# A planner's rough duration of a float32r TensorE pass, set to the measured one, in a two-layer hybrid trunk step

## The chip, the cores and the metric

One core of one Trainium2 chip. The metric is device time in microseconds (us), median of the runs shown. In views of the profile PE is TensorE's matmuls, PEld its weight loads, DVE is VectorE, ACT ScalarE, POOL GpSimd, SP SyncE.

## The reference, cut to what matters

Two trunk layers run over 128 context tokens and 256 latent tokens, 1024 wide (T = 384 tokens side by side in the kernel). Each layer is a macaron of three residual parts, every one modulated by nine vectors computed from a condition:

```
mod = silu(cond) @ w_mod[l] + b_mod[l]            # 1024 -> 9 * 1024, per layer and condition
x = x + 0.5*g1 * swiglu(m(rmsnorm(x)), w1, w3, w2)     # 1024 -> 2816 -> 1024
x = x + g2 * mixer_l(m(rmsnorm(x)))
x = x + 0.5*g3 * swiglu(m(rmsnorm(x)), w1, w3, w2)
```

The mixer of layer 0 (even) is a bidirectional gated linear recurrence beside differential attention of 4 heads; that of layer 1 (odd) is windowed grouped-query attention with 16 heads and sink logits. Both have one input and one output projection. Outputs are y for both token groups and the context keys, values and states.

## The kernel before, in words

**Layout.** x lies transposed: 8 tiles of 128 features by 384 tokens. A weight tile is 128 by 128. Every weight is split into a float32r high part (`hi`) and a low part (`lo`), and so is every x operand, and one product takes three float32r passes of 384 columns (386 where two columns for the shift ride along): hi*hi, hi*lo, lo*hi (`mm3`, line 436). Products of small operands inside the mixers (norm sums, gates, context scores, attention times values) are plain float32.

**Stages, in order.** The start computes the first modulation vectors. Then come `ffn(0,0)`, `even_mixer`, `ffn(0,1)`, `ffn(1,0)`, `odd_mixer`, `ffn(1,1)`. In the profiled execution they run at about 36 to 316, 316 to 482, 482 to 757, 757 to 1041, 1041 to 1188 and 1188 to 1460 us. An `ffn` (line 602) has an up pass of 22 tiles, each 16 `mm3` (48 passes) into one of two `sc` PSUM tiles, and a down pass of 8 tiles of 22 `mm3` (66 passes) into one of two `mm` PSUM tiles.

**Weights.** 156 chunks of 1 MB arrive on SP's queue in the order in which the program reads them (`w_load`, DMA on line 387). A group of 8 weight tiles is split by `w_split` (line 391): a 1024-column copy to `hi`, mostly on ACT, and a 1024-column subtraction to `lo` on DVE. Four groups are held; splitting runs three groups ahead of the matmuls.

**Modulation.** 128 tiles of `w_mod`, 0.5 MB each, arrive on POOL's queue, and DVE reduces each one twice (`mod_one`, line 476; tile `junk`, two conditions). Each reduction waits for `DVE_IDLE`, that is, it is written where the planner thinks that DVE has at most 0.6 us of work queued. These reductions are written during the FFNs only, up to tile 6 of the down pass.

**The order of the written program.** Each engine executes its instructions in the order written, and waits at the first whose inputs are missing. That order is chosen while the program is written. `Clock` (line 83) keeps a rough time at which each engine falls free and each tile is ready; `Eng.cost` (line 229) gives a rough duration for each instruction; a result is usable on another engine 0.2 us later (`HOP`). `Sched.now()` (line 127) is the planned time of TensorE. After each `mm3` or small matmul, `tick` (line 164) goes through the side chains (evacuations, norms, attention heads, weight splits, modulation) and writes up to six of their stages whose inputs are, on this clock, ready by `now()`. A side chain's own matmuls (call them pieces) are thus put between passes of the main stream. `ffn`, `proj_pass` and `out_pass` also ask the clock: from which tile on the normed x is used instead of the scaled x (`direct`), and which output tile comes next.

The lines of `cost` for TensorE and DVE, and of `tick`:

```python
        if self._name == "PE":
            if op == "transpose":
                return 0.109
            n = k["rhs"].free_size()
            if k["rhs"].dtype in (F32R, BF16):
                return n * 0.000417 + 0.0035
            us = max(n, 128) * 0.00168
            return us * max(out.shape[0], 32) / 128
...
        if op in self.SLOW:
            m = max([v.free_size() for v in ins] + [n]) if op != "tensor_tensor_reduce" else ins[0].free_size()
            return 0.065 + col + 0.00104 * m
...
    def tick(self):
        if not self.busy:
            n = 0
            while n < 6 and self._poll(self.now()):
                n += 1
```

Every compute instruction is issued through `Eng`, so nearly all rows of the profile have line 214; tiles tell them apart. Slab tiles are named `s` whatever they hold.

Names used below. `normed_all` (line 560) makes the normed x, eight features in turn, two SCALAR_TENSOR_TENSOR on DVE each, waiting for the norm (`RS.ev`) and `DVE_IDLE`. `evac` (line 687) empties an `mm` tile of the projection. `qk_norm` (line 714) has one piece of two passes against `cst`, and a shift by a DMA from `s` to `s` that the planner counts as 3.0 us. `a_chain` (lines 1099, 1182) writes scores, a maximum, exponentials, sums, and 128-column transposes against `ident`. `o_chain` (lines 1123, 1210) is attention times values.

Of the kernel before, what the change touches and what calls it, by code (L numbers as in the profile page):

```python
# [17 lines left out]
PSUM = bass.MemoryType.PSUM  # L18
# [27 lines left out]


class Event:
    """Something that a chain of instructions has still to emit, with the tiles that it leaves."""

    def __init__(self):
        self.tiles = None


class Banks:
    """PSUM tiles of one tag: how many may be in use at a time, and when the free ones fell free."""

    def __init__(self, n):
        self.at = [0.0] * n


class Idle:
    """Ready when an engine has nothing else queued."""

    def __init__(self, eng):
        self.eng = eng
# [14 lines left out]


class Clock:
    """Rough times of the engines while the program is written: they order the emission and nothing else."""

    def __init__(self):
        self.free = dict.fromkeys(("PE", "ACT", "DVE", "POOL", "DMA"), 0.0)
# [29 lines left out]


class Sched:
    """Emits the stages of side chains between pieces of the matmul stream, each when its inputs should be there."""  # L120

    def __init__(self):
        self.clock = Clock()
# [76 lines left out]


class Eng:
    """An engine's instructions, timed by the clock as they are written."""

    SLOW = {"tensor_tensor", "scalar_tensor_tensor", "tensor_tensor_scan", "tensor_reduce", "tensor_tensor_reduce"}

# [22 lines left out]
    def cost(self, op, out, ins, k):  # L229
        n = out.free_size()  # L230
        ps = any(v.space == PSUM for v in ins)
        if self._name == "PE":
            if op == "transpose":
                return 0.109
            n = k["rhs"].free_size()
            if k["rhs"].dtype in (F32R, BF16):
                return n * 0.000417 + 0.0035
            us = max(n, 128) * 0.00168
            return us * max(out.shape[0], 32) / 128
        if self._name == "ACT":  # L240
            extra = sum(0.093 for n_ in ("scale", "bias", "accum_out") if hasattr(k.get(n_), "tensor"))
            return 0.093 + 0.000833 * n + extra + (-0.042 if ps else 0.0)
        col = 0.064 if any(hasattr(v, "tensor") and v.free_size() == 1 for v in ins[1:]) else 0.0
        if self._name == "POOL":
            return 0.06 + 0.0007 * n
# [3 lines that stand above are left out]
        if op == "reciprocal":  # L249
            return 0.065 + 0.0083 * n  # L250
        return 0.065 + col + (0.00104 if ps else 0.00052) * n


def emit(tc, D, order):
    nc = tc.nc
    ctx = ExitStack()
    with ctx:
# [12 lines left out]
        clock = sched.clock  # L270
# [49 lines left out]
            S_.activation(out, in_, func, **kw)  # L320

        def copy(out, in_, scale=None):
            """out = in_ (times a column), on the engine that should be done with it first."""
            k = {} if scale is None else {"scale": scale}
            r = max(clock.at(in_)[0], clock.at(out)[0])
            ta = max(clock.free["ACT"], r) + S_.cost("activation", out, [in_], k)
            td = max(clock.free["DVE"], r) + V.cost("tensor_copy", out, [in_] if scale is None else [in_, scale], k)
            if td + ON_ACT < ta:
                if scale is None:
                    V.tensor_copy(out, in_)  # L330
                else:
                    V.tensor_scalar(out, in_, scale, None, ALU.mult)
            else:
                act(out, in_, AF.Copy, **k)

# [1 line left out]
        scT = cpool.tile([P, KD, 32], F32, name="scT")  # L337
        craw = cpool.tile([P, KD, 2], F32, name="craw")
        nc.sync.dma_start(craw, D["c_cols"])
# [8 lines left out]
        x = [sl() for _ in range(KD)]  # L348
# [19 lines left out]
            o = PPC[name][0] + i  # L368
            return pp[:, o:o + 1]

# [1 line left out]
        class WS:  # L372
            raw, hi, lo, rest = {}, {}, {}, {}
            asked, due = set(), []
# [69 lines left out]
            TE.matmul(ps, lhsT=lhsT, rhs=rhs, start=start, stop=stop)  # L444
            sched.tick()

# [1 line left out]
        M = {}  # L448
        mod_todo = [(0, k, t) for k in range(2, 9) for t in range(8)] + [(1, k, t) for k in range(9) for t in range(8)]
        mod_tiles = {}  # L450
# [23 lines left out]
                V.tensor_scalar(m, m, 0.5, None, ALU.mult)  # L474

        def mod_one():
            """Generator: one modulation tile, a condition per stage."""
            i = mod_at[0]
            l, k, t = mod_todo[i]
            mod_at[0] += 1  # L480
            if t == 0:
                M[l, k] = cpool.tile([P, 8, 2], F32, name=f"M{l}_{k}")
            w = mod_tiles.pop(i)
            for c in range(2):
                yield DVE_IDLE, w
                junk = modp.tile([P, 1024], BF16, tag="junk", name=nm("junk"), bufs=1)
                V.tensor_tensor_reduce(out=junk, in0=w, in1=cbc[:, c, :], scale=1.0, scalar=0.0,
                                       op0=ALU.mult, op1=ALU.add, accum_out=M[l, k][:, t, c:c + 1])
            mod_load()
            if t == 7:  # L490
                mod_finish(l, k)
                mod_done.add((l, k))
# [17 lines left out]
                sched.busy = was  # L510
            return M[l, k]

# [1 line left out]
        class XS:  # L514
            hi, lo, ev, sq, A, sh = [], [], [], None, None, None

# [3 lines left out]
            XS.hi, XS.lo, XS.sq, XS.ev = [None] * KD, [None] * KD, None, [Event() for _ in range(KD)]  # L520

        def prep(d, with_sh=True):
            """Generator: scaled x as two float32r parts, and the sum of squares."""
            q = sl()
            hi = XS.hi[d] = sl(F32R, TB)
            lo = XS.lo[d] = sl(F32R, TB)
            act(q, x[d], AF.Square)
            for r, c in RANGES:
                copy(hi[:, r], x[d][:, r], XS.A[:, d, c:c + 1])
            if with_sh:  # L530
                copy(hi[:, T:TB], XS.sh[:, d, :])
            yield hi, q
            if XS.sq is None:
                XS.sq = q
            else:
                V.tensor_tensor(XS.sq, XS.sq, q, ALU.add)
            for r, c in RANGES:
                V.scalar_tensor_tensor(lo[:, r], x[d][:, r], XS.A[:, d, c:c + 1], r32(hi[:, r]), ALU.mult, ALU.subtract)
            if with_sh:
                V.tensor_tensor(lo[:, T:TB], XS.sh[:, d, :], r32(hi[:, T:TB]), ALU.subtract)  # L540
            sched.fire(XS.ev[d], hi, lo, XS.sq)

        class RS:
            t, ev = None, None
# [13 lines left out]
            sched.add(gen(RS.t, RS.ev, XS.ev))  # L558

        def normed_all(low):  # L560
            """Starts the chains that leave the normed and modulated x as two float32r parts."""
            xn = [None] * KD
            xn_ev = [Event() for _ in range(KD)]
            A, sh, rs_ev, rs = XS.A, XS.sh, RS.ev, RS.t
# [33 lines left out]
                yield from prep(d)  # L598
            sched.add(gen())

# [1 line left out]
        def ffn(l, n, nxt):  # L602
            sched.fire(mod_on)
            gkind = 2 if n == 0 else 8
# [78 lines left out]
            h[0], h[1] = hh, hl  # L683
            sched.fire(h[2], hh, hl)

# [1 line left out]
        def evac(ps, direct):  # L687
            t = sl()
            if direct:
# [22 lines left out]
        sig_done = Event()  # L712

        def qk_norm(t, bc, gate, gs):
            """Generator: leaves the normed rows in t, then returns the two parts of the rotated ones."""
            sq = sl()
            if bc is None:
                act(sq, t, AF.Square)
# [102 lines left out]
            sched.add(gen())  # L821

        def transposed(src, n):
            """w (128 queries, n*128 keys) -> SBUF (keys, n, queries)."""
            pt = mst()
            for b in range(n):
                TE.transpose(pt[:, b * P:(b + 1) * P], src[:, b * P:(b + 1) * P], ident)
            w = sl()
            copy(w[:, :n * P], pt[:, :n * P])
            free(msb, pt, w)  # L830
            return w
# [13 lines left out]
            return ps, n  # L845

        def proj_pass(tiles, key, done, low):
            """Projection tiles in order; the first two share a K order that leaves the last tile of x late."""
            i = 0
            xn, xn_ev = normed_all(low) if low < 5 else (None, [Event() for _ in range(KD)])  # L850
            direct = False
# [27 lines left out]
                    i += 1  # L879

        def out_pass(key, gm, nxt, ready, free_at, early, wide):
            """Output projection. The K tiles in `early` come first: x takes their part while the others are computed."""
            prep_begin(*nxt)
            gm = mod_need(*gm)
            late = [k for k in range(KD) if k not in early]
# [3 lines left out]
            borrowed = set()  # L889

            def slot(t, ps):
                """A bank that has nothing to do: kept while there are units to come."""
                if todo:
                    slots.append((t, ps))
                else:
                    (msb if ps.tensor.name in borrowed else mmb).at.append(t)
# [61 lines left out]
            ready[k][0], ready[k][1] = hh, hl  # L958
            sched.fire(ready[k][2], hh, hl)

# [1 line left out]
        def even_mixer(nxt):  # L962
            mod_on.tiles = None
            rstd_chain()
# [203 lines left out]
            proj_pass(tiles, "e_in", done, XN_E)  # L1168
            out_pass("e_out", (0, 5), nxt, ready, [ready[k][2] for k in range(4, 8)], [4, 5, 6, 7], WIDE_E)

# [1 line left out]
        def odd_mixer(nxt):  # L1172
            mod_on.tiles = None
            rstd_chain()
# [65 lines left out]
            proj_pass(tiles, "o_in", done, XN_O)  # L1240
            out_pass("o_out", (1, 5), nxt, ready, [ready[k][2] for k in range(8)], list(range(O_EARLY)), WIDE_O)

# [1 line left out]
        def wm_load(i):  # L1244
            t = rawp.tile([P, 2, 1024], F32, tag="raw", name=nm("wm0"))
            nc.sync.dma_start(t, D["wm0"][i])
# [2 lines left out]

        def mixer_consts():  # L1250
            yield RS.ev, el, pp
            # differential lambda, negated
            V.tensor_scalar(gsub, par("subln"), 1.0 - LAM_INIT, None, ALU.mult)
            lj = sl()
            for m in range(2):
                V.tensor_tensor_reduce(out=lj[:, 0:64], in0=el[:, 2 * m, :], in1=el[:, 2 * m + 1, :], scale=1.0, scalar=0.0,
                                       op0=ALU.mult, op1=ALU.add, accum_out=ls[:, m:m + 1])
            # -8 * softplus(-lam) on (128, 2 directions, 4 tiles); log1p by its series in z / (2 + z)
            lam = pp[:, PPC["lam"][0]:PPC["lam"][0] + 8]
            V.tensor_scalar(sa, lam, -1.0, None, ALU.mult)  # L1260
            V.tensor_tensor(sb, lam, sa, ALU.min)
# [85 lines left out]
        sched.drain()  # L1347


# order of the 64 rows of a q or k head on the partitions: the two rows of a rotary pair side by side  # L1350
ROPE = np.array([b + i + s for b in (0, 32) for i in range(16) for s in (0, 16)])
UNROPE = np.argsort(ROPE)

# [133 lines left out]
```

## Time and profile before

| | |
|---|---|
| median of 3 runs | 1465.27 us (1465.2 to 1465.8) |
| profiled execution, span from first to last instruction | 1464.2 us (its own time is not listed apart from the runs) |
| TensorE busy | 1436.7 us, 98% |
| VectorE busy | 1115.4 us, 76% |
| ScalarE busy | 659.8 us, 45% |
| granted TensorE clock, mean | 0.997 |
| bytes moved by DMA | 250.67 MB, 171 GB/s |

How to read it: busy time is the time in which an engine had an instruction at work. A matmul's duration overlaps with the next one's, so the pace of the stream is read from how many passes stand in a stretch. The waits view lists time in which an engine had nothing at work, and what ended it. The windows view gives busy time of each engine in a stretch, with its instruction count in brackets.

### The profile page before, as it was taken

Reading aid. Unit: us, or ns where it says so; the run is one execution under the profiler, and the core shown is the slowest. Engines: PE = TensorE matmul, PEld = TensorE weight load, DVE = VectorE, ACT = ScalarE, POOL = GpSimd, SP = SyncE. Lnnn points to the kernel's source line nnn. Section 1 sums busy time; section 2 is a strip of 40 time slices with the busy share of each in tenths; the row PEclk is TensorE's granted clock in tenths of the full one; section 3 lists DMA queues with packets and bytes.
Section 4 is the critical chain, followed back from the end, with each engine's and each line's share of the span. In section 5 each row is a group of like instructions: output and inputs, shape, how many; then the busy total and the mean of one; then the engine's idle time right before and its main releaser. Section 6 shows DMA issues by size and latency. Waiting matters only on the chain.

```text
span 1464.2 us, 21823 instructions
## 1 busy us (share of the span) xinstructions
PE 1436.7 (98%) x8354; PEld 1398.4 (96%) x8354; DVE 1115.4 (76%) x2103; ACT 659.8 (45%) x1193; POOL 103.8 (7%) x214
## 2 busy tenths in 40 slices
PE   4999999999999999999999999999999999999998
PEld 1999999998889999999999999999998899999998
DVE  3899999969998998999979997444698795444332
ACT  3643333348875633333345333333477664333321
POOL 0001111110220011111100110000100000000000
PEclk9999999999999999999999999999999999999999
DMA  9557767652322366766744766333331233333430
GB/s 361 216 185 257 246 245 257 235 173 101 120 99 97 140 230 236 254 243 231 254 177 153 251 243 196 135 119 130 117 107 51 77 120 115 133 126 116 146 135 22
DMA packets 49560, 250.67 MB, mean 171 GB/s; under 512 B 6464, under 2 KB 10960, under 8 KB 28336
## 3 DMA queue, kind: packets, MB, share of 16 engines
q1 hardware_dynamic: 29664, 180.05, 34.0%
q0 software_dynamic: 19792, 69.23, 14.2%
q8 instruction: 66, 1.08, 0.3%
q14 instruction: 38, 0.31, 0.1%
HBM read 244.53 MB, written 2.36 MB: 169 GB/s over the span
## 4 chain that ended last, share of the span: by engine, by line
PE 95%; DMA 2%; DVE 2%; ACT 1%; issue 0%; SPq 0%; DVEq 0%; ACTq 0%
PE sc L214 54%; PE mm L214 36%; PE ms L214 5%; DVE s L214 1%; DMA wm<-in_wm 1%; DMA s<-in_xT 1%; DMA raw<-in_wst 0%; DVE lo L214 0%; ACT s L214 0%; DMA s<-s 0%; ACT hi L214 0%; ACT L317 0%; SPq L737 0%; SPq L1296 0%; DVEq L1434 0%
## 5 line engine op out<-in xcount | busy, mean ns | idle before, releaser
L214 PE MATMUL sc<-s,hi 128*128 128x384 f32 (+1 forms) x2816 | 726.3, 339 | 2.3 <-ACT s L214 1.4
L214 ACT ACTIVATE hi<-raw 128x1024 fp32r<-128x1024 f32 x298 | 315.7, 1060 | 541.7 <-PE sc L214 307.4
L214 DVE TENSOR_TENSOR lo<-raw,hi 128x1024 fp32r<-128x1024 f32 x312 | 381.3, 1223 | 231.2 <-ACT hi L214 230.0
L214 PE MATMUL mm<-s,hi 128*128 128x384 f32 (+1 forms) x2072 | 545.8, 344 | 2.3 <-DVE s L214 2.3
L214 PEld LDWEIGHTS sc<-s,hi 128*128 128x128 f32 x2816 | 512.6, 188 | 5.0 <-ACT s L214 1.8
L214 PE MATMUL sc<-s,lo 128*128 128x384 f32 (+1 forms) x1408 | 475.4, 338 | 0.0
L214 PEld LDWEIGHTS mm<-s,hi 128*128 128x128 f32 x2072 | 372.9, 188 | 12.4 <-issue 3.0
L214 PE MATMUL mm<-s,lo 128*128 128x384 f32 (+1 forms) x1036 | 349.1, 337 | 0.0
L214 DVE CUSTOM_DVE_ANT_0 junk<-wm,cbc 128x1024 bf16<-128x1024 f32 x256 | 312.6, 1221 | 11.0 <-DMA wm<-in_wmt 8.3
L214 PEld LDWEIGHTS sc<-s,lo 128*128 128x128 f32 x1408 | 265.0, 188 | 0.0
L214 PEld LDWEIGHTS mm<-s,lo 128*128 128x128 f32 x1036 | 194.7, 188 | 0.0
L214 ACT ACTIVATE s<-s 128x384 f32<-128x384 f32 (+3 forms) x215 | 108.0, 507 | 171.9 <-DVE s L214 157.0
L214 DVE TENSOR_TENSOR s<-s,s 128x384 fp32r<-128x384 f32 (+6 forms) x214 | 112.0, 528 | 20.0 <-ACT s L214 18.9
L214 POOL DMA_DIRECT2D wm<-in_wmt x126 | 66.6, 528 | 695.1 <-DVE M L214 674.2
L214 DVE SCALAR_TENSOR_TENSOR s<-s,M,s 128x128 fp32r<-128x128 f32 (+3 forms) x256 | 92.4, 416 | 3.8 <-ACT s L214 3.7
L214 ACT ACTIVATE s<-s,M 128x256 fp32r<-128x256 f32 (+1 forms) x167 | 66.3, 446 | 11.0 <-DVE s L214 8.1
L214 DVE SCALAR_TENSOR_TENSOR s<-mm,M,s 128x128 f32<-128x128 f32 x104 | 38.5, 412 | 32.2 <-PE mm L214 32.2
L214 DVE TENSOR_TENSOR s<-sc,s 128x384 f32<-128x384 f32 x106 | 56.8, 551 | 0.0
L214 PE MATMUL sc<-s,s 128*128 128x384 f32 (+2 forms) x208 | 49.0, 373 | 0.7 <-ACT s L214 0.7
L214 ACT ACTIVATE s<-ms 128x384 f32<-128x384 f32 (+3 forms) x80 | 31.8, 423 | 29.8 <-PE ms L214 29.5
L214 PEld LDWEIGHTS sc<-s,s 128*128 128x128 f32 x208 | 34.1, 189 | 7.0 <-ACT s L214 1.3
L214 ACT ACTIVATE s<-sc,sm 128x385 f32<-128x385 f32 (+3 forms) x72 | 35.9, 511 | 0.0
(107 smaller groups left out, 635.1 us busy)
## 6 DMA issues: line engine op xcount, KB each, us to landing
raw<-in_wst SPq DMA_DIRECT2D x156, 1024.0 KB, 5.0
wm<-in_wmt POOLq DMA_DIRECT2D x126, 512.0 KB, 3.8
wm<-in_wm SPq DMA_DIRECT2D x8, 1024.0 KB, 7.6
s<-s SPq DMA_DIRECT2D x36, 64.0 KB, 2.4
s<-in_xT SPq DMA_DIRECT2D x8, 192.0 KB, 7.4
out_y<-s SPq DMA_DIRECT2D x8, 192.0 KB, 1.9
cbc<-in_c_rows SPq DMA_DIRECT2D x1, 1024.0 KB, 8.4
wm<-in_wmt SPq DMA_DIRECT2D x2, 512.0 KB, 9.7
```

The costliest lines, as they stand in the source:

```text
L214: r = fn(*a, **k)
```

## The change

One line of `Eng.cost` (line 237), the planned duration of a matmul whose moving operand is float32r or bfloat16:

```diff
             if k["rhs"].dtype in (F32R, BF16):
-                return n * 0.000417 + 0.0035
+                return n * 0.0004375 + 0.007
```

For 384 columns that is 163.6 ns before and 175.0 ns after. The rest of the diff empties docstrings and comments, line for line, so that line numbers stay. No instruction's shape, engine or operands are edited; what can differ is the order in which instructions are written, which of `hi`'s copies go to ACT or DVE (`copy`, line 322, compares the two engines' planned free times), from which tile the normed x is used, and which output tiles are taken in one or two parts.

## Rows read from the trace of the kernel before

**Rows 1.** The page: span; busy us (share) and instructions of each engine.
```profile
span 1464.2 us, 21823 instructions
PE 1436.7 (98%) x8354; PEld 1398.4 (96%) x8354; DVE 1115.4 (76%) x2103; ACT 659.8 (45%) x1193; POOL 103.8 (7%) x214
```
**Rows 2.** Waits of TensorE: waiter, releaser, us in total, times, longest.
```profile
PE mm L214 <- DMA wm<-in_wm: 16.7, 8, 6.6
PE mm L214 <- DVE s L214: 2.3, 2, 2.0
PE sc L214 <- ACT s L214: 2.1, 2, 1.4
PE ms L214 <- DVE s L214: 1.2, 2, 0.6
PE sc L214 <- DVE s L214: 0.9, 2, 0.5
PE ms L214 <- ACT s L214: 0.6, 2, 0.4
```
**Rows 3.** Windows: stretch, length, busy us (instructions) of PE to POOL, clock, DMA, GB/s.
```profile
0.00:36.00 36.00, 16.53 (x133) 5.53 (x133) 12.09 (x36) 12.68 (x36) 2.19 (x10) 0.95 0.94 360
...
318.00:330.00 12.00, 10.01 (x55) 9.46 (x54) 9.56 (x32) 7.39 (x14) 0.00 (x0) 1.00 0.25 89
466.00:482.00 16.00, 15.60 (x89) 15.15 (x88) 15.78 (x44) 13.30 (x36) 0.00 (x0) 1.00 0.29 111
482.00:665.00 183.00, 183.00 (x1039) 182.72 (x1040) 172.03 (x287) 75.25 (x109) 17.96 (x34) 1.00 0.64 224
1041.00:1061.00 20.00, 19.36 (x105) 17.76 (x103) 11.81 (x26) 12.58 (x22) 4.21 (x10) 1.00 0.35 124
1110.00:1160.00 50.00, 49.02 (x381) 43.30 (x380) 43.17 (x120) 34.67 (x100) 0.00 (x0) 1.00 0.17 61
1460.00:1464.20 4.20, 0.50 (x3) 0.17 (x1) 0.74 (x2) 0.00 (x0) 0.00 (x0) 0.80 0.13 47
```
**Rows 4.** Chain that ended last: start us, us, what; the first FFN's down pass.
```profile
223.97 93.96 PE mm L214 x538
```
**Rows 5.** Windows of the DVE reductions (tile junk): busy us (instructions), clock, DMA share.
```profile
482.00:665.00 183.00, 86.60 (x71) 1.00 0.64 224
```
**Rows 6.** Timeline across one up tile: start us, us, instruction [idle before].
```profile
107.20 1.23 DVE L214 TENSOR_TENSOR lo<-raw,hi 128x1024 fp32r<-128x1024 f32 x1 [0.41 <-ACT hi L214]
108.34 0.55 DVE L214 TENSOR_TENSOR s<-sc,s 128x384 f32<-128x384 f32 x1
...
115.48 0.47 ACT L214 ACTIVATE s<-sc 128x384 f32<-128x384 f32 x1
```
**Rows 7.** Timeline at the even mixer's start, DVE and PE.
```profile
323.89 2.72 DVE L214 SCALAR_TENSOR_TENSOR s<-s,M,s 128x128 f32<-128x128 f32 x8 [1.22 <-ACT s L214]
...
326.63 0.55 DVE L214 TENSOR_TENSOR s<-mm,s 128x384 f32<-128x384 f32 x1
...
327.32 0.59 PE L214 MATMUL mm<-s,hi 128*128 128x386 f32 x2 [1.99 <-DVE s L214]
```
**Rows 8.** Timeline: two pieces in the mixers, each with what precedes it.
```profile
430.69 0.20 ACT L214 ACTIVATION_READ_ACCUMULATOR s<-sc,sm 128x1 f32 x1
...
430.96 0.89 PE L214 MATMUL sc<-s,s 128*128 128x384 f32 x2
...
1125.63 0.82 PE L214 MATMUL ms<-ident,s 128*128 128x128 f32 x6
...
1126.71 0.55 PE L214 MATMUL ms<-ident,s 128*128 128x128 f32 x3 [0.25 <-ACT s L214]
```
**Rows 9.** Chain that ended last: the odd mixer's first norm piece.
```profile
1048.05 0.59 ACT s L214
...
1052.76 3.66 DMA s<-s
...
1060.50 0.91 PE ms L214 x2
```

## The prediction

> **What bounds the kernel now.** I read the page first. TensorE is busy for 1436.7 of 1464.2 us [rows 1], so 27.5 us is all that any new order could win from its idle time. The windows say where that idle time lies [rows 3]. The first 36 us hold 19.5 us of it (36.00 less 16.53), the last 4.2 us hold 3.7, and four short stretches hold the part in between: 1.99 us at the start of the even mixer (318 to 330), 0.40 where the FFN after it begins (466 to 482), 0.64 at the start of the odd mixer (1041 to 1061) and 0.98 inside that mixer (1110 to 1160). These four sum to 4.0 us. The waits view agrees: 16.7 us are for the first modulation weights, and all other waits together are 7.1 us [rows 2], of which about 3 lie in the start. In the FFNs the stream is solid, with 183.00 busy of 183.00 us in an up pass [rows 3].
>
> The pace inside the stream comes from the chain view: 538 passes in 93.96 us, 174.6 ns each [rows 4]. The planner counts 163.6 ns now and 175.0 after. So the plan of before runs TensorE 6.5% too fast (163.6/175.0 = 0.935), and the plan after runs it right. DVE is the second engine: 172.03 busy of 183.00 us in that up pass, 15.78 of 16.00 where the even mixer ends [rows 3].
>
> **The change, part by part.** It removes and adds no operation. What it moves is the place in the TensorE stream at which stages of side chains are written: a chain that takes L us on ACT and DVE was planned to span L/0.1636 passes and now spans L/0.175. Its pieces come up to 6.5% of L earlier in the stream, and reductions of modulation fill 6.9% more planned time per pass of TensorE.
>
> *Passes.* Their number is fixed by the loops, and the stream's pace is the hardware's. Cost 0. A tile that moves to the normed x drops from 386 to 384 columns, too little to count.
>
> *Start and end.* Both are plain float32 matmuls, loads, and the last store; their planned costs are not edited, and the 19.5 and 3.7 us stay. Cost 0.
>
> *FFNs.* The plan of before believed an up pass of 183 us to last 171 (183/1.0695); now it has 12 us more room on DVE, which it fills with reductions at its own 1.13 us (0.065 + 0.00104 x 1024), some 10.6 more. A reduction really takes 86.60/71 = 1.22 us [rows 5], so 12.9 us more on a DVE that has 183.00 - 172.03 = 11.0 us idle. DVE ends the pass about 2 us late, 3 with its small read-outs. What hides this: an up tile is emptied by DVE at 108.89 (108.34 + 0.55), and its PSUM tile is wanted again only when the next up tile is done, which ACT's first read of that one shows at 115.48 [rows 6]. That is 6.6 us of cover. The `lo` tiles are split three groups ahead (72 passes, 12.6 us). Cost 0; if the cover were gone, 2 to 3 us in each of three up passes, 6 to 9. POOL's loads move with the reductions, at 0.64 of the DMA engines' time [rows 5], and SP's loads are paced by TensorE, so no queue is late. The modulation is finished earlier, which costs nothing.
>
> *Start of the even mixer.* TensorE waits 1.99 us because the projection's first evacuation (326.63) stands on DVE behind eight SCALAR_TENSOR_TENSOR of `normed_all` (2.72 us, four features, 0.66 each as the plan has it) [rows 7]. These were written first because in the plan the norm is ready before the tile is. Between the last FFN pass and that tile's end stand 45 passes, 0.51 us more in the new plan. A feature pair takes 0.66, so whole pairs: none or one more. Ends: +0.66, and -1.99 if the evacuation goes first. I take 0, as 0.51 is short of a pair.
>
> *Pieces that already wait.* The odd mixer's first norm piece waits until 1060.50, because the shift DMA in its chain takes 3.66 us [rows 9] and the plan says 3.0. From the ACT step at 1048.05 to the piece lie 12.4 us, of which some 66 passes; written 66 x 0.0114 us earlier, the piece waits 0.75 us longer. The transposes at 1126.71 wait for a copy begun by the transposes at 1125.63 [rows 8], a chain of 1.1 us: +0.07. The rest of the 0.98 us of idle time in that window [rows 3] is taken alike: +0.1. Sum +0.9.
>
> *Pieces that just do not wait.* The mixers hold about 144 pieces by the loops (36 score groups, 66 transposes groups, 18 head norms, 12 outputs, 8 gates, 4 output norms). One such stands 0.07 us behind its input (input done at 430.89, piece at 430.96) [rows 8]. With a chain of 3 us, between those above, a piece comes 0.2 us earlier. Low end 0 (one wait makes all later inputs relatively earlier, as the stream stands still while ACT and DVE go on), high end one in five waiting 0.2 us, 5.8 us. I take 0, near the trace's own state, where only three or four pieces wait at all.
>
> Sum: +0.9 us on a span of 1464.2; the median of 1465.27 is that span and 1.1 us around it. So 1466.2 us.
>
> The rule that speaks against the change is in the Trainium skill, "TensorE: Matmul & The Clock Gate", section "Wait — 56ns, not 53.3ns?": back-to-back matmuls at the full clock start every N/2.4 GHz plus about 2.5 ns. For 384 columns an estimate by it is 162.5 ns, which is the old constant; the edit would then spoil a correct plan. The trace does not agree: 174.6 ns at a granted clock of 1.00 [rows 3, 4]; by the rule those 538 passes would take 87.4 us and not 93.96.
>
> **The rivals.** *Faster: the waits go.* With TensorE planned right, chains meet the stream where they really do. For it: the plan's DVE costs fit the trace (0.66 per pair), and the 1.99 us is a matter of order alone [rows 7]. Against it: the wait at 1060 is a DMA's, which the plan still counts too short, and most chains lose spare time. All four stretches gone give 1465.27 - 4.0 = 1461.3 us; a win of over 0.2% (2.9 us, about what a measurement of this kernel can tell from no change) needs three quarters of them.
>
> *Slower: the spare time was what kept pieces from waiting.* The plan's TensorE ran ahead of the real one, so every piece stood 6.5% of its chain behind its inputs. With that gone, one in five of 144 pieces waits 0.2 us: 1465.27 + 5.8 = 1471.1 us. It decides where a piece's input is done less than 0.2 us before it. For it: the piece at 430.96 with 0.07 us, DVE at 15.78 of 16.00 [rows 3, 8]. Against it: waits in one in-order stream give time to those behind them.
>
> *The order does not matter.* The new order differs, but at no place that TensorE waits for: 1465.3 us. For it: TensorE works in 98% of the span already [rows 1], and the waits hang on a few places.
>
> *A pass is really 163.6 ns, and the new plan is too slow.* Then all 144 pieces come 0.2 us early with no spare time left, 144 x 0.2 = 28.8 us, and 1494 us. The 93.96 us of rows 4 speak against it.
>
> **How the numbers follow.** The forecast has a chance of 0.54 (its own range is 1464.2, where the 1.99 us goes as well, to 1468.2, where one piece in ten waits, 14 x 0.2 = 2.9 us over 1465.27), the indifferent order 0.07, faster 0.13, slower 0.25, the wrong pass 0.01. Faster by over 0.2% is the rival at 1461.3: 0.13. Within 0.2% are forecast and indifferent order: 0.61. Slower by over 0.2% is 0.26. The range takes in the faster rival's floor, 1461.3, and upwards the slower rival's price, 1471.1, rounded to 1471; what lies outside is more than one in five waiting pieces, or DVE running late beyond its cover, about 0.15.
>
> **What would show it.** Right: TensorE busy within 2 us of 1436.7; some 76 reductions in 482 to 665 us where 71 were [rows 5]; up passes with no idle TensorE; idle time of 3 to 8 us in the two mixers, more of it on `ms` and `sc` pieces. Wrong: a wait on `lo` or on an `sc` evacuation inside an FFN (the cover of 6.6 us was not there); the even mixer's first evacuation ahead of `normed_all` (the faster rival); or reductions written inside a mixer, which would put 1.22 us each on DVE at its fullest.

## The result and the profile after

The changed kernel takes 1480.77 us (1479.2 to 1482.71, four runs) beside 1465.24 us (1464.87 to 1465.8, four runs) for the one before on the same chip. The ratio is 1.0104 (95% interval 1.009 to 1.0118), so the change made the kernel 15.5 us slower. The forecast was 1466.2 us, and its range ended at 1471.0.

The page of the kernel after, its span, busy times and the summary of the chain that ended last:

```profile
span 1480.8 us, 21818 instructions
PE 1442.1 (97%) x8354; PEld 1397.9 (94%) x8354; DVE 1114.1 (75%) x2106; ACT 648.3 (44%) x1183; POOL 103.5 (7%) x214
...
PE 69%; DVE 10%; DMA 9%; issue 9%; ACT 1%; POOL 0%; SPq 0%; DVEq 0%; POOLq 0%
```

TensorE does the same 8354 instructions as in [rows 1], and DVE does no more than before (1114.1 against 1115.4 us). What is new is in the chain: a tenth of it each now runs through DVE, the DMAs and stretches in which nothing is seen to be waited for. The profiled execution is 16.6 us longer than the one before; it is the longest of the four.

The waits of TensorE after (waiter, releaser, us in total, times, longest):

```profile
PE mm L214 <- DMA wm<-in_wm: 17.4, 8, 6.2
PE mm L214 <- DVE s L214: 5.9, 5, 2.7
PE ms L214 <- DVE s L214: 4.1, 5, 2.1
PE mm L214 <- DVE lo L214: 1.9, 2, 1.0
PE sc L214 <- DVE s L214: 1.9, 4, 0.7
PE sc L214 <- ACT s L214: 1.6, 2, 1.4
PE ms L214 <- ACT s L214: 1.1, 2, 0.8
PE mm L214 <- ACT s L214: 0.6, 1, 0.6
```

Beside the first modulation weights they sum to 17.1 us where [rows 2] had 7.1. Nearly all of the increase is released by DVE.

Where it lies is read from windows cut at the `ms<-s,ones_d` matmuls, the norm sums between the stages. Both tables have the order first FFN, even mixer, second FFN, third FFN, odd mixer, last FFN (the first row from 36 us on, when the start is over); the columns are those of [rows 3]. Before:

```profile
36.00:320.81 284.81, 284.49 (x1612) 283.89 (x1613) 259.24 (x475) 115.16 (x172) 30.18 (x57) 0.99 0.65 231
320.81:483.44 162.63, 160.25 (x876) 146.64 (x875) 151.05 (x349) 122.99 (x277) 21.69 (x49) 1.00 0.30 105
483.44:762.27 278.83, 278.83 (x1587) 278.56 (x1587) 254.91 (x431) 107.89 (x163) 27.48 (x52) 1.00 0.64 224
762.27:1041.29 279.02, 279.02 (x1588) 278.75 (x1588) 195.48 (x325) 108.19 (x161) 15.81 (x32) 1.00 0.49 172
1041.29:1188.02 146.73, 145.10 (x1012) 133.18 (x1012) 123.99 (x321) 98.79 (x261) 6.49 (x14) 1.00 0.25 87
1188.02:1460.00 271.98, 271.98 (x1553) 271.71 (x1553) 117.92 (x168) 94.14 (x128) 0.00 (x0) 1.00 0.33 116
```

After:

```profile
36.00:324.69 288.69, 285.21 (x1613) 283.55 (x1613) 264.60 (x484) 111.14 (x170) 32.27 (x61) 0.99 0.66 235
324.69:492.84 168.15, 162.77 (x867) 145.61 (x866) 151.41 (x347) 122.68 (x274) 21.57 (x49) 0.99 0.29 101
492.84:774.27 281.43, 280.07 (x1597) 279.00 (x1597) 261.99 (x447) 104.00 (x163) 29.04 (x55) 1.00 0.64 228
774.27:1051.81 277.54, 277.54 (x1587) 277.27 (x1587) 180.38 (x300) 104.96 (x157) 12.10 (x25) 1.00 0.46 159
1051.81:1203.89 152.08, 147.77 (x1011) 134.29 (x1011) 123.92 (x321) 99.36 (x261) 6.36 (x14) 0.99 0.24 82
1203.89:1476.60 272.71, 272.71 (x1552) 272.44 (x1552) 118.48 (x169) 93.03 (x127) 0.00 (x0) 1.00 0.33 117
```

Length less busy time is TensorE's idle time. It was nil in all FFNs but for 0.3 us; now the first FFN has 3.5 us of it and the second 1.4, the even mixer 5.4 (2.4 before) and the odd one 4.3 (1.6 before). The counts matter as well: nine or ten instructions of the even mixer now stand behind the mark at its end. At 174.6 ns each [rows 4] they are about 1.6 us, which belong to the mixer's length. So the first FFN lost 3.9 to 4.3 us (288.69 less 284.81, or counted from the first FFN's own opening mark as in the table below), the even mixer about 7, the second FFN about 1, the odd mixer 5.4. The third FFN is 1.5 us shorter and the last 0.7 longer with no idle time in either kernel; differences of that size have no waits behind them, and nothing is read from them below.

Idle time understates a wait. A pass's record lasts 337 ns on average (`sc<-s,lo` on the page after) while passes start every 174.6 ns, so a stall of up to some 0.16 us shows as busy time. Of the even mixer's 7.1 us, 3.0 are idle time and 4.1 are busy time with the same number of matmuls; 1.5 of these are a stretch at half the clock, shown further down.

### The profile page after: what moved, and what is told of

Same layout as the page of the kernel before. It is cut to its first block, busy times and chain, and to the rows that moved or that the text cites. A ratio compares the mean times of both kernels' runs of the same rounds, so it can differ in the third digit from the quotient of the medians.

```text
span 1480.8 us, 21818 instructions
## 1 busy us (share of the span) xinstructions
PE 1442.1 (97%) x8354; PEld 1397.9 (94%) x8354; DVE 1114.1 (75%) x2106; ACT 648.3 (44%) x1183; POOL 103.5 (7%) x214
## 4 chain that ended last, share of the span: by engine, by line
PE 69%; DVE 10%; DMA 9%; issue 9%; ACT 1%; POOL 0%; SPq 0%; DVEq 0%; POOLq 0%
PE sc L214 45%; PE mm L214 21%; DMA wm<-in_wmt 7%; DVE s L214 5%; PE ms L214 4%; DVE lo L214 2%; DVE junk L214 2%; DVE sm L214 1%; DMA wm<-in_wm 1%; DMA s<-s 1%; DMA s<-in_xT 0%; DMA raw<-in_wst 0%; ACT s L214 0%; ACT hi L214 0%; POOL wm L214 0%
## 5 line engine op out<-in xcount | busy, mean ns | idle before, releaser
L214 ACT ACTIVATE hi<-raw 128x1024 fp32r<-128x1024 f32 x294 | 308.0, 1056 | 372.2 <-PE sc L214 219.7
L214 ACT ACTIVATE s<-s 128x384 f32<-128x384 f32 (+4 forms) x215 | 108.3, 507 | 362.2 <-DVE s L214 343.5
```

The lines of the kernel that those rows point to most:

```text
L214: r = fn(*a, **k)
```

## The experiments

The theory after the result: two separate losses, one in the FFNs and one in the mixers, both because stages of side chains are written earlier in the TensorE stream than their inputs are really there. The rivals: one loss, in the FFN or at the even mixer's start, which is carried on; or a loss that is spread evenly, so that any shift of the pace costs in proportion. The table holds the profiled execution of each kernel: us of each stage between the same marks as above, with 0.1746 us added for each matmul that stands on the other side of a mark than before. It is worked out from the traces, one execution each; the runs e1 to e14 are described one by one below it. How far two executions of one order differ can be read from it too: in the odd mixer TensorE's instructions stand in the same order in the kernel after, e2, e3 and e9, and that mixer took 152.1, 150.2, 149.2 and 149.6 us; the first FFN, in one order in the kernel after, e1 and e5 to e9, took 286.8 to 289.4 us.

```
                     FFN   even   FFN   FFN    odd   FFN
before             283.7  162.6 278.9 279.0  146.7 272.2
after              288.0  169.7 280.1 277.5  152.1 272.9
e1_ffn_only        288.6  162.8 281.2 278.2  146.7 272.0
e2_mixers_only     284.1  168.2 278.8 278.2  150.2 272.9
e3_land            283.4  169.7 278.4 277.6  149.2 273.0
e4_half            284.8  165.0 277.9 278.9  147.9 272.4
e5_spare           288.1  164.9 279.5 278.0  150.3 271.9
e6_shift           289.4  167.0 279.2 278.1  149.6 272.9
e7_dve             286.8  165.9 281.4 278.4  150.0 273.0
e8_act             288.8  169.5 279.7 278.3  148.2 272.1
e9_gate_after      286.9  164.2 280.7 278.9  149.6 271.5
e10_gate_before    284.9  169.1 277.8 278.2  146.7 272.6
e11_fast           284.1  199.3 278.6 277.6  148.6 272.6
e12_all            284.4  167.0 278.3 279.1  150.7 272.5
e13_act_odd        284.5  164.0 278.5 278.7  148.1 271.7
e14_both           284.7  172.7 278.8 279.5  148.9 273.1
```

**The new duration in one kind of stage only.** `in_ffn` is set where `ffn` begins and taken back where a mixer begins.

```diff
-                return n * 0.0004375 + 0.007
+                return n * 0.0004375 + 0.007 if self._clock.in_ffn else n * 0.000417 + 0.0035
```

> The planned pass is 175.0 ns (for 384 columns) while the four FFNs are written and 163.6 ns in the two mixers. In the changed kernel the norm piece that opens the even mixer stands 3.9 us later than before, the first pass of the second FFN 9.4, of the third 12.0, of the odd mixer 10.5, of the last FFN 15.9: so the FFNs lose some 5.7 us and the mixers some 10.9. Theory A (each stage loses by itself): 1465.2 + 6 = 1471 us, even mixer 163 us long as before. Theory B (only the mixers' pieces lose, and the FFN waits are small change): 1466 to 1467 us. Theory C (DVE is late when it leaves the FFNs and carries this into the mixers): about 1480 us.

With the new value in the FFNs alone: 1472.48 us, ratio 1.0037 (1.0024 to 1.005), +5.7 us over the 1466.74 us of before. The other way round:

> The reverse: 175.0 ns in the two mixers, 163.6 ns in the FFNs. Theory A: 1465.2 + 11 = 1476 us. Theory B: 1479 us. Theory C: 1465 to 1466 us, since DVE enters the mixers as before.

With the new value in the mixers alone: 1475.35 us, 1.0057 (1.0042 to 1.0072), +8.6 us. The two sum to 14.3 us, beside 15.5 for the whole change. In the table the first two FFNs of the one and the mixers of the other bear the loss, and what they leave alone is as before, to about 1 us. So there are two losses, each made where the plan was edited; a loss that is carried on falls.

**When a modulation tile is counted as landed.** `mod_load` (line 454) counts a tile's 512 KB as landed about 3.5 us after DVE's planned free time. This adds 1.5 us, on the changed kernel:

```diff
             landed(t, 1 << 19, clock.free["DVE"])
+            clock.ready[t.tensor.name] = (clock.free["DMA"] + 3.5, "DMA")
```

> The changed kernel, with the planner counting 1.5 us more until a modulation tile has landed, so that a reduction is written later behind its load; all else as in the changed kernel. If DVE stood still at the head of its queue for these loads (36.6 us in 32 waits after, 8.3 in 11 before) and this made the FFNs lose: those waits fall to below 10 us, the waits of TensorE inside the FFNs' down passes go, and the time falls by 4 to 6 us to 1475 to 1477. If the FFNs lose because DVE has too much work, not for the loads: no change, 1480 us. If theory C holds: 1466 us.

1475.16 us, 1.0055 (1.0038 to 1.0072). The first FFN falls from 288.0 to 283.4 us and the second from 280.1 to 278.4: the whole loss of the FFNs in the profiled executions. What DVE waited for in the first FFN, the two largest rows each (waiter, releaser, us, times, longest), before:

```profile
DVE lo L214 <- ACT hi L214: 17.1, 21, 3.0
DVE junk L214 <- DMA wm<-in_wmt: 2.9, 5, 1.2
```

After:

```profile
DVE junk L214 <- DMA wm<-in_wmt: 17.2, 15, 2.6
DVE lo L214 <- ACT hi L214: 3.0, 4, 1.6
```

With the later landing time:

```profile
DVE lo L214 <- ACT hi L214: 11.8, 14, 3.0
DVE junk L214 <- DMA wm<-in_wmt: 3.4, 3, 1.9
```

The two rows sum to some 20 us in both kernels; DVE's idle time in that stage changed its cause. Before, DVE idled at a `lo` for ACT's `hi`, while the modulation loads landed. After, reductions were written closer together, and DVE stands with one at the head of its queue until its load is there. The timeline of the kernel after, in the first FFN's down pass (start us, us, instruction, idle before), shows who is behind it:

```profile
287.28 0.53 POOL L214 DMA_DIRECT2D wm<-in_wmt  x1 [6.67 <-DVE M L214]
...
292.22 1.22 DVE L214 CUSTOM_DVE_ANT_0 junk<-wm,cbc 128x1024 bf16<-128x1024 f32 x1 [1.40 <-DMA wm<-in_wmt]
...
293.38 0.74 DVE L214 SCALAR_TENSOR_TENSOR s<-mm,M,s 128x128 f32<-128x128 f32 x2
...
294.26 0.42 PE L214 MATMUL mm<-s,hi 128*128 128x384 f32 x1 [1.56 <-DVE s L214]
```

The load was issued at 287.28, and its reader could start at 292.22, 4.9 us later. DVE lost 1.40 us there; behind the reduction stood the read-out of an `mm` tile (293.38), and TensorE, which needs that tile for the next output, waited 1.56 us. The other two waits of that FFN, 1.9 us (`DVE lo` in the table of waits), are for `lo` splits; the first, at 306.35, has two reductions ahead of it on DVE, and the earlier of these stood 1.65 us for its load. With the later landing time the stretch from 36 to 318 us is solid again, with 282.00 of 282.00 us busy. The edit also moved some reductions out of that FFN (DVE is busy for 260.8 us of it, 264.0 after and 258.2 before, counted between the marks of the table), so a small part may be DVE's work and not its queue:

```profile
36.00:318.00 282.00, 282.00 (x1604) 281.39 (x1603) 260.03 (x468) 113.17 (x168) 31.35 (x59) 1.00 0.66 236
```

**Half of the step.** The constant midway, 169.2 ns for 384 columns:

```diff
-                return n * 0.0004375 + 0.007
+                return n * 0.000427 + 0.00525
```

> The planned pass halfway, n * 0.000427 + 0.00525 (169.2 ns for 384 columns), everywhere. If the loss is a trend (spare time of every piece shrinks with the constant): about half of it, 1472 to 1474 us. If waits begin only once the spare time is used up: under a third of it, 1466 to 1470. If any new order costs as much by accident: anywhere from 1465 to 1481, and no order among the constants.

1470.26 us, 1.0036 (1.0023 to 1.0049); six of its ten runs lie at 1469.6 to 1470.4 and four at 1473.5 to 1476.0, and the profiled one is of the six. In that execution the FFNs are as before, within 1.1 us, and the even mixer has 2.4 us more. So the FFNs' loss sets in beyond this point, and the mixers' before it; where the four longer runs lose is not known. The median is 3.5 us above before, the ratio gives 5.3: between the two answers that were expected.

**The other direction.** A pass of 153.6 ns in the plan, shorter than in either kernel:

```diff
-                return n * 0.0004375 + 0.007
+                return n * 0.0004
```

> The planned pass at n * 0.0004, 153.6 ns for 384 columns, everywhere: as far below the kernel before as the changed one lies above it, nearly. If the loss comes from spare time alone, a faster planned TensorE gives pieces more of it: waits in the mixers fall from the 7.1 us listed before to about 5, and the time to 1463 to 1465 us. If the kernel before stands at a best point between pieces that come too early and results that come too late: slower, 1467 to 1472 us.

1503.51 us, 1.0259 (1.0245 to 1.0274): +38 us over the 1465.67 of before, 36.7 of it in the even mixer. Both expectations, 1463 to 1465 and 1467 to 1472, missed. A stretch near that mixer's end, and the wait in it:

```profile
448.00:472.00 24.00, 4.27 (x13) 3.87 (x14) 20.53 (x43) 5.25 (x9) 2.64 (x5) 0.57 0.48 165
```

```profile
466.14 0.69 PE L214 MATMUL mm<-s,hi 128*128 128x384 f32 x1 [19.86 <-ACT s L214]
```

With a plan that runs TensorE too fast, the last chains of the mixer are written so late that the output projection waits 19.9 us for them. The time is thus not a matter of more or less shift: 153.6 ns gives +38 us, 163.6 ns (before) 0, 169.2 ns +3.5 to +5, 175.0 ns +15.5. A loss in proportion to the shift falls too. That the kernel before stands at a point to which the rest of the plan was tuned, so that another order costs whichever way it differs, is a reading that these runs leave open: none of the versions here was faster.

**Spare time given back to all stages of the mixers.** On the changed kernel, a stage is written only 0.3 us after its planned time:

```diff
-            while n < 6 and self._poll(self.now()):
+            while n < 6 and self._poll(self.now() - (0.0 if self.clock.in_ffn else 0.3)):
```

> The changed kernel, but in the two mixers a side stage is written only when its inputs have been ready, on the plan's clock, for 0.3 us. Theory M (pieces in the mixers lost their spare time and TensorE now waits for each a little): most of the mixers' loss comes back; even mixer from 168.1 to 163 to 165 us, odd from 152.1 to 147 to 149, the whole 1480.8 to 1472 to 1475 (the FFNs keep their 5 us). Theory D (DVE as a whole is late against the plan, which a fixed delay does not mend): less than a third comes back, 1478 or more.

1475.44 us, 1.0061 (1.0044 to 1.0078). The even mixer falls from 169.7 to 164.9 us, the odd one from 152.1 to 150.3. Some 1.5 of the even mixer's 4.8 us are the half-clock stretch, which this execution does not have; the kernel of e2, with the order of the kernel after and no such stretch, took 168.2 us. What the 0.3 us did for the rest can be counted from matmul start to matmul start in the traces. Over the pace at which each kind of matmul follows where nothing holds it up, the starts of pieces in the even mixer are late by some 4.6 us more in the kernel after and in e2 than before, and by about 1 us more in e5; TensorE's wait of 2.7 us at the mixer's start is still there. So most of the even mixer's loss is of pieces written too early, as the theory says. The odd mixer's 150.3 us lies among the 149.2 to 152.1 that it takes without the edit: no gain is shown there, and the expected 147 to 149 was missed.

**Single costs of the plan in the mixers**, each on the changed kernel: the shift DMA as 4.5 us instead of 3.0, DVE's instructions 7% longer, ACT's instructions 7% longer.

```diff
-            clock.ready[sq.tensor.name] = (clock.at(t)[0] + 3.0, "DMA")
+            clock.ready[sq.tensor.name] = (clock.at(t)[0] + 4.5, "DMA")
```

```diff
+            if self._name == "DVE" and not self._clock.in_ffn:
+                us *= 1.07
```

> The changed kernel, with the rotary shift's DMA counted as 4.5 us and not 3.0 by the plan. If the mixers lose because DVE stands at the head of its queue for that DMA (DVE waits for s<-s 5.5 us after, 2.7 before) and everything behind it is late: even and odd mixer come back by 3 us and more each, the whole to 1474 us or less. Theory M: little, 1479 to 1481.

> The changed kernel, with every planned DVE duration in the mixers 7% longer, so that DVE stands to TensorE in the plan as before. Theory D: the mixers return to about 163 and 147 us, the whole to 1471 us. If it is ACT's results that come late, or the hand-over between engines: little, 1478 or more. Theory M gives about half, 1475.

> The changed kernel, with every planned ACT duration in the mixers 7% longer. Theory D: no gain, 1479 to 1482 us. If ACT is the late one: the mixers return, 1471 us. Theory M: about half, 1475.

The shift: 1478.64 us, 1.0082 (1.0063 to 1.0101). DVE: 1479.56 us, 1.0084 (1.0067 to 1.0101). ACT: 1478.49 us, 1.0075 (1.006 to 1.009). Over the 1466.47 us of before that is +12.2, +13.1 and +12.0, so each alone gives back 2.4 to 3.5 us of the 15.5, little more than the intervals. DVE 7% longer takes 3.8 us from the even mixer (2.3 against e2), about half of its loss where theory D expected all of it. ACT 7% longer brings the odd mixer to 148.2 us, 1.0 us below the shortest of the four executions without it and 3.9 below the longest; the odd mixer of the other two, 149.6 and 150.0 us, lies among those four.

**The first evacuation of the even mixer.** The eight features of `normed_all` are held back until two tiles of the projection are emptied (in the FFNs the event is fired at once):

```diff
-                yield rs_ev, DVE_IDLE
+                yield rs_ev, xn_gate, DVE_IDLE
...
+                        if i == 1:
+                            sched.fire(XS.gate)
```

> The changed kernel, with the even mixer's normed x begun only once the first two projection tiles have been evacuated. TensorE's wait there (2.7 us at 331.86, behind eleven DVE instructions) should go, and with it the 3.4 us at half the clock that stand behind it in the changed kernel's trace (332.7 to 336.1), worth half of them: 1480.8 - 2.7 - 1.7 = 1476 us. If the half clock has nothing to do with that wait: 1478, and the half clock still there. If the wait only moves to the next tile: 1480.

On the changed kernel: 1475.85 us, 1.007 (1.0057 to 1.0083); the even mixer takes 164.2 us, 5.5 less than without it (4.0 less than in e2). What stood in the way is in the timeline of the kernel after at the even mixer's start:

```profile
327.77 3.38 DVE L214 SCALAR_TENSOR_TENSOR s<-s,M,s 128x128 f32<-128x128 f32 x10 [1.23 <-ACT s L214]
...
331.17 0.54 DVE L214 TENSOR_TENSOR s<-mm,s 128x384 f32<-128x384 f32 x1
...
331.86 0.59 PE L214 MATMUL mm<-s,hi 128*128 128x386 f32 x2 [2.65 <-DVE s L214]
```

Ten SCALAR_TENSOR_TENSOR ahead of the evacuation, where [rows 7] had eight, and 2.65 us of waiting where it had 1.99. With the gate the same wait is 0.28 us:

```profile
328.24 0.59 PE L214 MATMUL mm<-s,hi 128*128 128x386 f32 x2 [0.28 <-DVE s L214]
```

The gate took away more than this wait. Behind it, the kernel after has a stretch at half the granted clock (second row; the third is the stretch that follows, the first one of the odd mixer):

```profile
1138.20:1141.60 3.40, 3.13 (x11) 2.78 (x12) 3.33 (x11) 2.71 (x12) 0.00 (x0) 0.50 0.07 24
332.50:336.10 3.60, 3.60 (x13) 3.60 (x12) 3.49 (x10) 0.00 (x0) 0.00 (x0) 0.53 0.00 0
336.10:339.20 3.10, 3.10 (x19) 3.10 (x19) 3.03 (x6) 1.45 (x2) 0.00 (x0) 1.00 0.00 0
```

At 19 passes in 3.10 us, 13 would take 2.1 us and took 3.60: 1.5 us lost. In e2 the same passes in the same order, at a granted clock of 1.00, take 1.5 us less. The gate's execution has no such stretch.

**The same gate on the kernel before**, with the old constant:

> The same edit on the kernel before: the wait of 2.0 us at 327.32 goes; 1465.2 - 2 = 1463.3 us, faster than both kernels. If what is put off is missed later (the normed x comes later, one more tile takes the scaled x with its dearer evacuation): 1465 us.

1472.24 us (1468.6 to 1473.86), 1.0039 (1.0028 to 1.0051), slower; both expectations missed. The wait at the mixer's start went, from 1.99 to 0.28 us, but its even mixer takes 169.1 us, 6.5 more than without: near the mixer's end TensorE now waits 1.6 and 1.9 us where it did not wait before, and 3.4 us at half the clock follow. The chains of this order come late in the stream, as in the run with 153.6 ns, and holding back the normed x would make them later still; that is a reading of where the waits lie, and was not tried apart. The gate is no improvement by itself. It mends an order that the new duration made.

**All three remedies.** First the landing time, the gate and the 0.3 us:

> The changed kernel with the three edits that each took away a part of the loss: modulation tiles counted 1.5 us later, 0.3 us of spare time for side stages in the mixers, and the even mixer's first two evacuations ahead of the normed x. If the parts are separate: 1480.8 - 5.6 - 5.3 - 3 = 1467 us, about the time before, with the measured pass in the plan. If they overlap (one wait takes the place of another): 1470 to 1475.

1474.79 us, 1.0061 (1.0048 to 1.0074). The FFNs are whole, but the even mixer is at 167.0 us, more than with the 0.3 us (164.9) or the gate (164.2) alone. A wait of 1.85 us before the output projection, with a half-clock stretch behind it, is new there: too much delay, it seems, as in the run before. Then, without the 0.3 us, and with ACT 7% longer in the odd mixer alone:

```diff
+            clock.ready[t.tensor.name] = (clock.free["DMA"] + 3.5, "DMA")
...
+                yield rs_ev, xn_gate, DVE_IDLE
...
+            if self._name == "ACT" and self._clock.stage == "odd":
+                us *= 1.07
```

> The changed kernel with one edit for each stage that lost: modulation tiles counted 1.5 us later (FFNs), the first two evacuations ahead of the normed x (even mixer), planned ACT durations 7% longer in the odd mixer alone. If the causes are these three, by stage: FFNs as before, even mixer about 164 us, odd mixer about 147.6 as with ACT 7% longer everywhere: 1467 us at most 1468. If the odd mixer's gain came from another order in the stages ahead of it: odd mixer 149 to 150, 1469 to 1471.

1466.89 us (1466.01 to 1467.74, eleven runs) beside 1466.13 us, ratio 1.0003 (0.9994 to 1.0012). The whole loss is gone, to within the interval, with the measured duration of a pass left in. The windows of its two mixers:

```profile
320.68:484.74 164.06, 162.02 (x876) 146.27 (x875) 154.97 (x362) 121.76 (x271) 21.52 (x49) 1.00 0.30 104
...
1041.88:1189.45 147.57, 145.34 (x1008) 132.50 (x1008) 125.22 (x323) 96.72 (x258) 6.43 (x14) 1.00 0.24 84
```

They idle 2.0 and 2.2 us, and the even mixer has its 876 instructions again. No version beat the kernel before.

**Both engines slower in both mixers**, so that the ratio of the three engines in the plan is again about that of the kernel before:

```diff
+            if self._name in ("ACT", "DVE") and self._clock.stage != "ffn":
+                us *= 1.07
```

> The changed kernel with modulation tiles counted 1.5 us later and planned DVE and ACT durations both 7% longer in the mixers, so that all three engines stand to one another as in the plan before; hand-over times are not scaled. If only the ratio of the planned engines counts: mixers of 162.6 and 146.7 us as before, 1466 us. If the 7% of TensorE alone explains less than that (hand-overs, fixed DMA times): 1468 to 1472.

With the landing time but no gate: 1476.25 us, 1.0077 (1.0063 to 1.0091), above both expectations. The even mixer takes 172.7 us, the most of any but the 153.6 ns plan; the profiled execution, at 1480.8 us, is the longest of its four by 4.4 us and has two half-clock stretches in that mixer. Restoring the ratio alone does not restore the order of before. That DMA times and the hand-over of 0.2 us were not scaled with it is one possible reason, and was not tried.

## Why the prediction was wrong

**What held.** The number of passes and the pace of the undisturbed stream did not change (the last FFN: 271.98 and 272.71 us). The up passes stayed solid (182.7 busy of 183.0 us in the second one). No reduction went into a mixer. Two of the prediction's signs came out larger than it gave them: both mixers idle more, but 9.7 us in all where 3 to 8 were expected, mostly for results of DVE, and TensorE is busy for 1442.1 us where 1436.7 within 2 were.

**"FFNs. Cost 0" was the first step to fail**, by the +5.7 us of e1. Two things were wrong in it. It looked for the added reductions in the up pass. The reductions (tile `junk`) after, in the up pass and the down pass of the first FFN and then of the second:

```profile
36.00:224.00 188.00, 83.38 (x69) 0.99 0.66 232
224.00:322.00 98.00, 45.92 (x38) 1.00 0.68 242
492.00:675.00 183.00, 86.56 (x71) 1.00 0.63 222
675.00:767.00 92.00, 47.60 (x39) 1.00 0.65 236
```

Before:

```profile
36.00:224.00 188.00, 79.78 (x66) 0.99 0.65 233
224.00:318.00 94.00, 39.93 (x33) 1.00 0.66 231
...
665.00:757.00 92.00, 40.41 (x34) 1.00 0.64 229
```

The second up pass kept its 71 [rows 5], where the step has 10.6 more and the prediction's list of signs has 76, which do not agree with each other; the first got 69 for 66, and the down passes got 38 for 33 and 39 for 34. And the step took DVE's busy time for the price, with the 6.6 us of cover of an up tile [rows 6]. The price was in the main not work (DVE is idle for 24.1 of the 288.7 us of the first FFN after) but a queue: DVE, with time to spare in the plan, came to a reduction before its load had landed, 17.2 us in all, and in the down pass the read-outs of `mm` tiles and the `lo` splits stand behind it. The 12.6 us of lead that the step gave the `lo` tiles did not hold: a wait on `lo` in an FFN is the sign of being wrong that the prediction named itself. That a load needs 4.9 us from issue to use where the plan counts about 3.5 from the time DVE falls free was harmless before: DVE waited 2.9 us for such loads in the first FFN, and TensorE for nothing of it. "POOL's loads move with the reductions" was in the text; that DVE would wait for them was not. The price "if the cover were gone", 6 to 9 us, was nearly right in size, by luck, as it was for three up passes and the waits came in the down passes of two FFNs; the range left it out.

**"Start of the even mixer: I take 0" was the second.** The end that was priced and not taken, one feature pair more, is what came: 2.65 for 1.99 us, the +0.66 exactly. That 0.51 us is short of a pair was no reason for 0: pairs come whole, so a shift of 0.51 of 0.66 us can bring the next one, and e4, with half the shift, has the ten SCALAR_TENSOR_TENSOR and a wait of 2.63 us already.

**"Pieces that just do not wait: I take 0" was the third.** The rival of lost spare time was the right mechanism, and had a chance of 0.25 and a price of 5.8 us. The mixers alone cost 8.6 us. In the even mixer the late starts of pieces (4.6 us more, 1 us more with 0.3 us of spare time) show the mechanism; of these 4.6 us the list of waits has 1.8, in four waits. The argument against it, that a wait gives time to those behind it, was too strong, and "only three or four pieces wait at all" was read from a list that leaves out stalls below some 0.16 us.

**The third norm piece** (the prediction called it the first; two stand ahead of it) does wait longer, 0.82 for 0.37 us, which is 0.45 of the 0.75 expected:

```profile
1071.00 0.91 PE L214 MATMUL ms<-s,cst 128*128 128x384 f32 x2 [0.82 <-ACT s L214]
```

**A term was missing:** the half clock, 1.5 us for the stretch at 332.5 and 1.2 at 1138.2 (against e9, which has the same order there at full clock), 2.7 us of the profiled execution's loss. The second follows the longest wait of the odd mixer:

```profile
1138.13 0.67 PE L214 MATMUL ms<-ident,s 128*128 128x128 f32 x2 [2.06 <-DVE s L214]
```

Most of that wait is a transfer's. DVE stood 1.54 us for the shift DMA ahead of it, with the operations for the transposes behind that in its queue (the transfer in the chain that ended last, then DVE's timeline):

```profile
1129.64 4.96 DMA s<-s
```

```profile
1134.63 0.42 DVE L214 TENSOR_TENSOR s<-s,cst 128x256 f32<-128x256 f32 x1 [1.54 <-DMA s<-s]
```

In e9, with the same order, the transfer takes 3.62 us, DVE stands 0.19 us for it, and TensorE 0.7:

```profile
1124.97 3.62 DMA s<-s
```

The plan counts 3.0 us. So here too DVE comes to the head of its queue before a load does, and how long that lasts differs from one execution to the next. TensorE's waits on `ms` for DVE in this mixer, 2.1 us after, were 1.3 us in e2, 0.4 in e3 and 0.7 in e9, none of which edits the odd mixer's costs further, and the mixer took between 149.2 and 152.1 us. So up to 3 us of its loss come and go between executions of one order, and the rest, 2.5 us or more, came with the new duration in each of them. ACT planned 7% longer there (148.2 us in e8, 148.1 in e13) takes 1.0 to 2.1 us from what e2, e3 and e9 have and leaves some 1.4; what the rest hangs on, and why ACT and not DVE is the engine to be corrected, was not settled.

**The faster rival** failed by its own condition: the norm's features did not move behind the first evacuation but one pair more moved ahead of it. **The rival of a wrong pass duration** stays excluded: where nothing waits, the pace is the old one.

## What to carry to other kernels

A constant of a planner is tuned together with the errors around it: setting one of them to its measured value took away a margin of 6.5% that had covered modulation loads counted some 1.5 us too short and, in the even mixer, chains written with no room to spare. Before correcting one, look for what its error was covering, and correct those together (the landing time, one order at a hand-over, one engine's costs), which here gave the old time and no more. When more work is pulled forward on an engine that runs in order, ask first whether the work's own inputs arrive that early, and what stands behind it in the queue.

## What the runs showed of the hardware

The granted TensorE clock fell to 0.5, that is from 2.4 to 1.2 GHz, in two stretches of 3.4 us in the middle of the kernel after, shortly after TensorE had stood still: at 332.68 us after the wait of 2.65 us, and at 1138.22 us after that of 2.06 us. The wait of 1.99 us in the kernel before brought none. It is not a matter of the wait's length alone, as e2 shows, which has the same wait of 2.65 us and a full clock behind it:

```profile
328.16 0.59 PE L215 MATMUL mm<-s,hi 128*128 128x386 f32 x2 [2.65 <-DVE s L215]
```

```profile
329.00:332.50 3.50, 3.50 (x22) 3.50 (x21) 3.39 (x10) 0.00 (x0) 0.00 (x0) 1.00 0.00 0
```

Nine of the profiled executions have this wait at 2.63 to 2.66 us; four of them have a half-clock stretch beside it (after, e3, e8, e14) and five have none (e2, e4, e5, e6, e7). In e1 and e10 one follows a wait of 1.78 and of 1.87 us. What makes the difference stays open. Its practical side is that a wait of some 2 to 3 us on TensorE may cost 1.5 us more than it lasts, and that two executions of one order can differ by that much.
